# Gated DeltaNet's input weights: the second part of a tile made by an accumulating DMA instead of a VectorE subtraction

## The chip, the cores and the metric

The kernel runs on one core of one Trainium2 chip. The metric is the device time of one execution in microseconds (us), as the median of three runs. A profile of one execution goes with it: every instruction with its start, duration and the source line it came from, and every DMA.

The core's engines each take their own instructions in order. TensorE (PE in the profile, with its weight loads as PEld) multiplies, VectorE (DVE) and ScalarE (ACT) work elementwise, GpSimd (POOL) does small copies and issues some DMAs, and SyncE (SP) issues the other DMAs. They wait for each other through semaphores.

## The reference

Four decoder layers on 1024 positions of width 1024, in float32. The layers use HGRN2, sliding-window attention, gated DeltaNet and HGRN2 again. Only the third is touched:

```python
def gdn_mixer(h, w_in, w_out, conv_w, a_log, dt_bias, onorm_g):
    qkv, z, a, b = jnp.split(h @ w_in, [GD_QKV, GD_QKV + GD_VW, GD_QKV + GD_VW + GD_V_HEADS], axis=-1)
    qkv = jax.nn.silu(causal_conv(qkv, conv_w))
    q, k, v = jnp.split(qkv, [GD_QKW, 2 * GD_QKW], axis=-1)
    ...
    o = gated_delta_scan(q, k, v, beta, g)
    o = rmsnorm(o, onorm_g).reshape(B, T, GD_VW).astype(h.dtype)
    return (o * jax.nn.silu(z)) @ w_out
```

`h @ w_in` is the projection whose weights the change concerns: 1024 rows and 6176 columns, of which 6144 go through the loader described below.

## The kernel before

**Two-part products.** A float32 product is made of three fast TensorE matmuls. Each operand is split into a first part `hi`, the value rounded to the type `fp32r`, and a second part `lo`, what the rounding left. `mm3` (lines 215 to 220) adds three products: first parts by first parts (L218), the weight's first part by the activation's second (L219), and the weight's second part `w_lo` by the activation's first (L220).

**The weight loader.** `load_w` makes one tile of 128 partitions by 512 elements, 256 KB. SP fetches the raw tile into `w_raw` (L187), ACT writes `w_hi` (L189), and DVE writes `w_lo` = raw − hi (L190). There are three buffers for `w_raw`, which the tiles `ada_w` of another stream share, and four for each of `w_hi` and `w_lo`. Where a scale is given (output weights), L192 and L193 do the same; they are not changed.

**Projections.** `proj_fm` takes a column block of 128 outputs. Its weights are two tiles of four contraction steps each. For each half of the positions (512) it runs 8 steps of `mm3`, so 24 matmuls, 12 for each tile; then an evacuation reads the result from PSUM. Blocks of k, q and v go through a convolution (`conv`, L684 to L697), with small POOL copies of the three columns at a half's border (L678, L680, L687: `gd_xs`, `gd_halo`). Some blocks are run for both halves with one load of the weights, others for one half at a time: of the 64 block loads, 32 serve two halves and 32 serve one. That makes 128 tiles and 96 halves.

**Units.** DeltaNet's 16 heads are done in 8 units of two. For each unit `inverse` solves a triangular system: 31 steps of two DVE instructions (L837, L838), then a chain of small matmuls into `z_ps` (L866 to L894) with copies by ACT, DVE and POOL between them (POOL's are L860, L861, L870 and L886, on `gd_Z` and `gd_uq`). `scan` then steps through the eight chunks of 128 positions (L934 to L969), a chain of TensorE, DVE and ACT. `weave` mixes the instructions of a unit's scan, the next unit's inverse, the projections of later units, and `side`, which prepares the next layer's modulation with DVE (L444, reading `ada_w`).

**Order.** The program is written through a tile framework. It gives each instruction its engine, inserts the semaphores, and orders the instructions of each engine by priority and by the time at which it plans them to be ready. An instruction moved from one engine to another therefore changes the planned order on all of them. On the chip each engine then works through its list strictly in order.

The stage of the change runs from about 1077 us (first raw tile fetched, while the layer before still ends) to about 1890 us of the profiled span; the last DeltaNet unit and the output projection follow.

Of the kernel before, what the change touches and what calls it, by code (L numbers as in the profile page):

```python
# [10 lines left out]
F32 = mybir.dt.float32  # L11
# [4 lines left out]
AF = mybir.ActivationFunctionType  # L16
ALU = mybir.AluOpType
# [30 lines left out]
def drain(g):  # L48
    for _ in g:
        pass  # L50


def chain(*gs):
    for g in gs:
        yield from g


def take(g, n):
    for _ in range(n):
        c = next(g, None)  # L60
        if c is None:
            return
        yield c


def weave(tc, *streams):

    live = [[g, tot, b, e - b, b, pr] for g, tot, b, e, pr in streams]
    while live:
        s = min(live, key=lambda x: x[4])  # L70
        if s[5]:
            with tc.high_priority(offset=s[5]):
                c = next(s[0], None)
        else:
            c = next(s[0], None)
        if c is None:
            live.remove(s)
        else:
            s[4] += c * s[3] / s[1]


class Trunk:
    def __init__(self, ctx, tc, ins):
        self.ctx, self.tc, self.nc, self.ins = ctx, tc, tc.nc, ins
        pool = lambda name, bufs=1, **k: ctx.enter_context(tc.tile_pool(name=name, bufs=bufs, **k))
        self.const = pool("const")
        self.big = pool("big")
        self.wp = pool("wp")
        self.adap = pool("adap")
        self.sm = pool("sm")  # L90
        self.ps = pool("ps", space=PSUM)
        self.np_, self.pb, self.pw, self.pe = 0, 3, 0, 0
        self.dram = pool("dram", space=bass.MemoryType.DRAM)
        self.xd = self.dram.tile([D, T], F32, name="xd")
        self.od = [self.dram.tile([D * (1 + n), T], F32, name=f"od{n}") for n in range(2)]
        self.pd = self.dram.tile([D, T], F32, name="pd")
        self.zd = self.dram.tile([2 * D, T], F32, name="zd")
        self.hhi, self.hlo = [None, None], [None, None]
        self.x = [None, None]
        self.oo, self.pre, self.last, self.parts, self.due, self.more = {}, {}, iter(()), 0, set(), True  # L100
        self.piece = self.hold = self.turn = self.step = None


    def hslot(self, name):
# [71 lines left out]
    def load_w(self, src, scale=None, pool=None):  # L176

        nc, pool = self.nc, pool or self.wp
        shape = list(src.shape)
        raw = self.wp.tile([P, HT], F32, name="w_raw", tag="raw", bufs=RAW)  # L180
        hi = pool.tile([P, HT], F32R, name="w_hi", tag="whi", bufs=WB)
        lo = pool.tile([P, HT], F32R, name="w_lo", tag="wlo", bufs=WB)
        raw, hi, lo = (x[:, :math.prod(shape[1:])] for x in (raw, hi, lo))
        if len(shape) == 3:
            raw, hi, lo = (x.rearrange("p (a b) -> p a b", a=shape[1]) for x in (raw, hi, lo))
        with self.tc.high_priority(offset=self.pw):
            nc.sync.dma_start(raw, src)  # L187
            if scale is None:
                nc.scalar.copy(hi, raw)  # L189
                nc.vector.tensor_tensor(lo, raw, hi.bitcast(F32), ALU.subtract)  # L190
            else:
                nc.scalar.activation(hi, raw, AF.Copy, scale=scale)  # L192
                nc.vector.scalar_tensor_tensor(lo, raw, scale, hi.bitcast(F32), ALU.mult, ALU.subtract)  # L193
            n = self.tc.cur_priority
        self.tc.cur_priority = n + self.pw
        return hi, lo
# [379 lines left out]
    def gdn(self, i, side):  # L576
        nc, ins = self.nc, self.ins
# [6 lines left out]
        def tl(tag, dt=F32):  # L584
            return gp.tile([P, HT], dt, name=f"gd_{tag}", tag=tag, bufs=bufs[tag])
# [6 lines left out]
        raw = self.wp.tile([P, HT], F32, name="w_raw", tag="raw", bufs=RAW)[:, :KT * 32].rearrange("p (k n) -> p k n", k=KT)  # L592
# [119 lines left out]
        def proj_kq(u, dd, halves=((0, 1),)):  # L712

            if not dd:
                dd.update(k=[0, 0], q=[0, 0], kt=[0, 0], v={})
                dd["ms"] = gp.tile([P, 2 * C], F32, name="gd_ms", tag="ms", bufs=2)

            def ev_k(hf, ps):
                dd["k"][hf] = tl("k")
                conv(dd, hf, ps, 8 + u, dd["k"][hf])  # L720

                def turn():
                    pt = trans(dd["k"][hf], "ktr_ps")
                    dd["kt"][hf] = tl("kt")
                    nc.scalar.copy(dd["kt"][hf], pt)
                    sumsq(dd, pt, hf * NC)

                return turn

            def ev_q(hf, ps):  # L730
                dd["q"][hf] = tl("q")
                conv(dd, hf, ps, u, dd["q"][hf])
                return lambda: sumsq(dd, trans(dd["q"][hf], "qtr_ps"), C + hf * NC)

            for hv in halves:
                yield from self.proj_fm(w_in, D + u * P, ev_k, hv)
                yield from self.proj_fm(w_in, u * P, ev_q, hv)
                if hv == (0,):
                    yield from proj_z(u, dd, hv)
                    return  # L740
            self.turns()
            t8 = lambda name, n=C: gp.tile([P, n], F32, name="gd_" + name, tag=name, bufs=2 if name in ("r2", "gn") else 3)
            ms = dd["ms"]
            nc.vector.tensor_scalar(ms, ms, 0.25, EPS, ALU.mult, ALU.add)
            r = self.rsqrt(ms, 2 * C, "g", gp)

            ir, r2, sc = t8("ir"), t8("r2"), t8("sc")
            gm, gn, gw = (t8(n, 2 * C) for n in ("gm", "gn", "gw"))
            ac = lambda x: x.rearrange("p (a c) -> p a c", a=2)
            hs = slice(2 * u * C, 2 * (u + 1) * C)  # L750
            nc.vector.tensor_tensor(ir, ms[:, :C], r[:, :C], ALU.mult)
            nc.vector.tensor_tensor(r2, r[:, :C], r[:, :C], ALU.mult)
            nc.vector.scalar_tensor_tensor(ac(gm), r2[:, None, :].to_broadcast([P, 2, C]), 0.25, ac(beta[:, hs]), ALU.mult, ALU.mult)
            nc.vector.tensor_scalar(gn, gm, -1.0, None, ALU.mult)
            nc.vector.tensor_tensor(gw, gm, wl[:, hs], ALU.mult)
            nc.vector.tensor_scalar(sc, r[:, C:], 0.5 * P ** -0.5, None, ALU.mult)
            dd.update(ir=ir, gm=gm, gn=gn, gw=gw, sc=sc)
# [19 lines left out]
        def proj_z(u, dd, halves=(0, 1)):  # L777
            for a in range(2):
                def ev(hf, ps):
                    th = tl("tb")  # L780
                    nc.scalar.activation(th, ps, AF.Tanh, scale=0.5)
                    nc.vector.scalar_tensor_tensor(th, th, 1.0, ps, ALU.add, ALU.mult)
                    nc.sync.dma_start(place(self.zd, 2 * u + a, hf), th)

                yield from self.proj_fm(w_in, 4 * D + (2 * u + a) * P, ev, halves)
# [187 lines left out]
        w_out, od, on = ins["gd_out_w"][0], self.od[1], self.par[:, 74:75]  # L973
        ds = [dict() for _ in range(U)]
        self.parts = 4
        self.early(chain(proj_kq(0, ds[0], ((0,),)), proj_z(1, ds[1], (0,)), proj_z(2, ds[2], (0,))), EV)
        drain(self.last)
        decays()
# [4 lines left out]
        for u in range(U):  # L983
            cs = [proj_z(x, ds[x], hv) for x, *hv in ZL[u]]
            tot = 10400 * sum(len(z) - 1 for z in ZL[u])
            if u + 2 < U:
                cs.append(proj_kq(u + 2, ds[u + 2]))
                tot += 20800
            if u + 1 < U:
                cs.append(proj_v(u + 1, ds[u + 1]))  # L990
                tot += 20800
            st_ = [(scan(u, ds[u]), 18000, 0, 1, PR[0])]
            if u + 1 < U:
                st_.append((inverse(u + 1, ds[u + 1]), 28000, 0, 1, PR[1]))
            else:
                self.fill_x(0)
                cs += [self.out_load(od, 0, KT, 0, gp, "tmp", 2, (self.zd, "tb", bufs["tb"])), self.out_mm(i, w_out, 0, KT, 0, on), self.out_load(od, 0, KT, 1, gp, "tmp", 2, (self.zd, "tb", bufs["tb"]))]
                tot += 41600
            weave(self.tc, *st_, (chain(*cs), tot, 0, 1, 0), (take(side, NS[2]), NS[2], 0, 1, 0))
        drain(side)  # L1000
        st.close()
        st = ExitStack()
# [637 lines left out]
```

## Time and profile before

| what | value |
|---|---|
| median of three runs | 2658.29 us (2656.97 to 2660.67) |
| profiled execution, from its first to its last instruction | 2664.1 us |
| granted TensorE clock, mean of the span | 0.990 |
| `w_lo` by DVE (L190) between 1090 and 1910 us | 128 instructions, 87.8 us |
| `w_hi` by ACT (L189) in the same stretch | 128 instructions, 79.7 us |
| DMAs issued by POOL in the whole program | 56: 48 of `xd` at L142 and 8 of the rotary tables |

The profiled span is 5.8 us (0.2%) above the median of the runs that were not profiled; the profile holds no time outside its span. The profile's page gives busy time by engine, the span in 40 slices, the DMA queues, the chain of work that ended last, and the costliest groups of instructions. A group's row ends with the idle time that its engine had just before it and with what ended that idle time. The trace answers further questions by stretch of time, by line and by wait. A matmul's end is modelled: neighbouring matmuls overlap in the records, so a PE that is shown busy can still be waiting a little.

### The profile page before, as it was taken

The page shows a single profiled execution, that of the slowest core. Times are in us where ns is not written, and L with a number is a line of the kernel's source. Part 1 is how long each engine was busy: PE and PEld are TensorE (multiplying, and loading weights), DVE is VectorE, ACT ScalarE, POOL GpSimd, SP SyncE. Part 2 cuts the span into 40 slices and gives each one's busy share as a digit, 9 for nine tenths or more (in the row PEclk, how much of TensorE's full clock was granted, in tenths as well). Part 3 has the DMA queues.
Part 4 walks back from the last instruction along what each step waited for, and adds up shares of the span by engine and source line. Part 5 has one row for each costly group of instructions (what it writes and reads, how often), then busy time and mean ns, then how long its engine had stood idle before and what let it go on. Part 6 is the DMA issues. An engine that isn't in the chain of part 4 may idle for free.

```text
span 2664.1 us, 50723 instructions
## 1 busy us (share of the span) xinstructions
PE 2568.7 (96%) x18271; PEld 2046.2 (77%) x18271; DVE 2021.6 (76%) x5655; ACT 1323.5 (50%) x3467; POOL 105.7 (4%) x278
## 2 busy tenths in 40 slices
PE   7999999999999999999999999999999999999998
PEld 4777777778888877677877777778688877787777
DVE  5585788687697877768899999988776837368675
ACT  4443444443464655545666666666544534345352
POOL 0001000001000000101000100110000000000000
PEclk8999999999999999999999999999999999999999
DMA  7333343544233253334343444333576412122343
GB/s 261 98 114 90 116 143 115 173 128 129 67 103 104 72 160 112 95 110 111 106 123 84 118 118 119 83 97 93 174 235 188 123 48 77 42 82 64 124 139 116
DMA packets 395025, 309.96 MB, mean 116 GB/s; under 512 B 74851, under 2 KB 314902, under 8 KB 394774
## 3 DMA queue, kind: packets, MB, share of 16 engines
q1 hardware_dynamic: 390550, 293.09, 37.4%
q0 software_dynamic: 4224, 13.64, 1.6%
q8 instruction: 144, 2.36, 0.4%
q14 instruction: 107, 0.88, 0.1%
HBM read 245.75 MB, written 60.88 MB: 115 GB/s over the span
## 4 chain that ended last, share of the span: by engine, by line
PE 72%; DVE 14%; DMA 6%; ACT 5%; issue 2%; SPq 1%; DVEq 0%; ACTq 0%
PE proj_ps L218 10%; PE proj_ps L220 10%; PE proj_ps L219 10%; PE outp_ps L218 4%; PE outp_ps L219 4%; PE outp_ps L220 4%; PE projw_ps L219 2%; PE projw_ps L218 2%; PE projw_ps L220 2%; DVE gd_tb L690 1%; DVE w_lo L190 1%; PE projt_ps L219 1%; PE projt_ps L220 1%; PE pv_ps L1502 1%; PE projt_ps L218 1%
## 5 line engine op out<-in xcount | busy, mean ns | idle before, releaser
L218 PE MATMUL proj_ps<-hhi,w_hi 128*128 128x512 f32 x1664 | 676.0, 407 | 3.7 <-ACT gd_tb L688 3.3
L219 PE MATMUL proj_ps<-hlo,w_hi 128*128 128x512 f32 x1664 | 671.4, 404 | 0.0
L220 PE MATMUL proj_ps<-hhi,w_lo 128*128 128x512 f32 x1664 | 671.1, 403 | 0.0
L218 PEld LDWEIGHTS proj_ps<-hhi,w_hi 128*128 128x128 f32 x1664 | 314.6, 189 | 64.3 <-ACT gd_tb L688 5.9
L220 PEld LDWEIGHTS proj_ps<-hhi,w_lo 128*128 128x128 f32 x1664 | 314.1, 189 | 58.1 <-issue 0.4
L219 PEld LDWEIGHTS proj_ps<-hlo,w_hi 128*128 128x128 f32 x1664 | 314.6, 189 | 55.2 <-issue 0.9
L189 ACT CAST w_hi<-w_raw 128x512 fp32r<-128x512 f32 x352 | 214.5, 612 | 270.5 <-PE proj_ps L219 150.8
L190 DVE TENSOR_TENSOR w_lo<-w_raw,w_hi 128x512 fp32r<-128x512 f32 x352 | 236.5, 676 | 138.2 <-ACT w_hi L189 135.2
L218 PE MATMUL outp_ps<-o_hi,w_hi 128*128 128x512 f32 x576 | 229.8, 401 | 7.9 <-ACT o_hi L1314 7.0
L219 PE MATMUL outp_ps<-o_lo,w_hi 128*128 128x512 f32 x576 | 229.6, 399 | 0.4 <-DVE o_lo L1315 0.2
L220 PE MATMUL outp_ps<-o_hi,w_lo 128*128 128x512 f32 x576 | 228.0, 398 | 0.5 <-DVE w_lo L193 0.4
L192 ACT ACTIVATE w_hi<-w_raw,par 128x512 fp32r<-128x512 f32 (+1 forms) x136 | 94.8, 698 | 131.0 <-PE outp_ps L219 88.1
L690 DVE SCALAR_TENSOR_TENSOR gd_tb<-gd_xs,taps,gd_tb 128x512 f32<-128x512 f32 x192 | 145.7, 759 | 16.2 <-ACT gd_tb L688 12.5
L218 PEld LDWEIGHTS outp_ps<-o_hi,w_hi 128*128 128x128 f32 x576 | 109.4, 190 | 31.8 <-ACT o_hi L1314 9.7
L193 DVE SCALAR_TENSOR_TENSOR w_lo<-w_raw,par,w_hi 128x512 fp32r<-128x512 f32 (+1 forms) x136 | 96.9, 715 | 45.2 <-ACT w_hi L192 43.9
L444 DVE SCALAR_TENSOR_TENSOR ada_acc<-ada_w,par,ada_acc 128x512 f32<-128x512 f32 x154 | 114.9, 746 | 19.8 <-DMA ada_w<-in_ada_w_dram 18.8
L219 PEld LDWEIGHTS outp_ps<-o_lo,w_hi 128*128 128x128 f32 x576 | 109.4, 190 | 24.9 <-DVE o_lo L1315 3.0
L220 PEld LDWEIGHTS outp_ps<-o_hi,w_lo 128*128 128x128 f32 x576 | 109.1, 190 | 22.6 <-DVE w_lo L193 1.1
L219 PE MATMUL projt_ps<-w_lo,hhi 128*128 128x256 f32 x384 | 111.6, 292 | 2.2 <-DVE w_lo L190 2.2
L218 PE MATMUL projt_ps<-w_hi,hhi 128*128 128x256 f32 x384 | 111.0, 292 | 2.7 <-ACT w_hi L189 2.7
L220 PE MATMUL projt_ps<-w_hi,hlo 128*128 128x256 f32 x384 | 111.4, 292 | 0.0
L218 PE MATMUL projw_ps<-w_hi,hhi 128*128 128x512 f32 x256 | 102.8, 407 | 2.3 <-DVE hg_q L1032 2.3
(409 smaller groups left out, 5218.0 us busy)
## 6 DMA issues: line engine op xcount, KB each, us to landing
ada_w<-in_ada_w_dram SPq DMA_DIRECT2D x160, 256.0 KB, 2.8
w_raw<-in_hg_in_w_dram SPq DMA_DIRECT2D x136, 256.0 KB, 2.9
w_raw<-in_gd_in_w_dram SPq DMA_DIRECT2D x128, 256.0 KB, 3.0
o_in<-od SPq DMA_DIRECT2D x72, 256.0 KB, 3.7
x<-xd SPq DMA_DIRECT2D x64, 256.0 KB, 4.4
w_raw<-in_gd_out_w_dram SPq DMA_DIRECT2D x64, 256.0 KB, 3.1
xd<-x POOLq DMA_DIRECT2D x48, 256.0 KB, 2.9
w_raw<-in_sw_in_w_dram SPq DMA_DIRECT2D x48, 256.0 KB, 3.1
```

The source lines that it names most:

```text
L189: nc.scalar.copy(hi, raw)
L190: nc.vector.tensor_tensor(lo, raw, hi.bitcast(F32), ALU.subtract)
L192: nc.scalar.activation(hi, raw, AF.Copy, scale=scale)
L193: nc.vector.scalar_tensor_tensor(lo, raw, scale, hi.bitcast(F32), ALU.mult, ALU.subtract)
L218: mm(out, a[0], b[0], start=start, stop=False)
L219: mm(out, a[0], b[1], start=False, stop=False)
L220: mm(out, a[1], b[0], start=False, stop=stop)
L444: self.step = self.nc.vector.scalar_tensor_tensor(acc, w, c, acc, ALU.mult, ALU.add)
L690: last = nc.vector.scalar_tensor_tensor(y, xs[:, j:j + HT], w(j), y, ALU.mult, ALU.add)
L1502: self.tied([lambda b=b, a=a: nc.tensor.matmul(po[a * 64:(a + 1) * 64], vg[:, n + 1 - nkb + b, :], p4s[b][:, :, a, :], start=b == nkb - 1, ...
```

## The change

For the tiles of `gd_in_w` that are loaded while DeltaNet runs, DVE no longer takes part. ACT writes `w_hi` as before, then writes the negated first part into `w_lo` (`activation` with scale −1.0), and POOL issues a DMA from SBUF to SBUF that adds the raw tile onto it. A flag, `by_dma`, is set before the first early projections and cleared after the last unit's loop, so the other layers' tiles and the output weights keep their way.

```diff
+        self.by_dma = False
...
             nc.sync.dma_start(raw, src)
-            if scale is None:
+            if scale is None and self.by_dma:
+                nc.scalar.copy(hi, raw)
+                nc.scalar.activation(lo, hi.bitcast(F32), AF.Copy, scale=-1.0)
+                nc.gpsimd.dma_start(lo, raw, accum_op=ALU.add)
+            elif scale is None:
                 nc.scalar.copy(hi, raw)
                 nc.vector.tensor_tensor(lo, raw, hi.bitcast(F32), ALU.subtract)
...
         self.parts = 4
+        self.by_dma = True
         self.early(chain(proj_kq(0, ds[0], ((0,),)), proj_z(1, ds[1], (0,)), proj_z(2, ds[2], (0,))), EV)
...
             weave(self.tc, *st_, (chain(*cs), tot, 0, 1, 0), (take(side, NS[2]), NS[2], 0, 1, 0))
+        self.by_dma = False
         drain(side)
```

The added lines shift the numbers: in the changed kernel the three new steps are L190 (`w_hi`), L191 (negated copy) and L192 (DMA), and DeltaNet's lines are 5 higher (L837 is L842).

On DVE, inside the first inverse (`gd_A` holds the system, `gd_Tb` its growing inverse, `gd_tmp` the products), two `w_lo` stood among the steps. Before:

```order
L837 TENSOR_TENSOR gd_tmp<-gd_A,gd_Tb 128x121
L190 TENSOR_TENSOR w_lo<-w_raw,w_hi 128x512
L838 TENSOR_TENSOR gd_Tb<-gd_Tb,gd_tmp 128x11x11
L697 SCALAR_TENSOR_TENSOR gd_k<-gd_tb 128x512
L837 TENSOR_TENSOR gd_tmp<-gd_A,gd_Tb 128x110
L838 TENSOR_TENSOR gd_Tb<-gd_Tb,gd_tmp 128x10x11
L837 TENSOR_TENSOR gd_tmp<-gd_A,gd_Tb 128x108
```

After:

```order
L842 TENSOR_TENSOR gd_tmp<-gd_A,gd_Tb 128x121
L843 TENSOR_TENSOR gd_Tb<-gd_Tb,gd_tmp 128x11x11
L842 TENSOR_TENSOR gd_tmp<-gd_A,gd_Tb 128x110
L843 TENSOR_TENSOR gd_Tb<-gd_Tb,gd_tmp 128x10x11
L695 SCALAR_TENSOR_TENSOR gd_tb<-gd_xs,taps,gd_tb 128x512
L842 TENSOR_TENSOR gd_tmp<-gd_A,gd_Tb 128x108
```

The tile's instruction is gone from between the steps, and the convolution's instructions (L690, now L695; L697) stand elsewhere among them.

On ACT, around the fourth inverse's copy of `gd_Tc` (L848, now L853), the change puts a second instruction for each tile, with others between the two. Before:

```order
L189 CAST w_hi<-w_raw 128x512
L770 ACTIVATE gd_v<-vtr_ps,gd_ir 128x128
L848 COPY gd_Tc<-gd_tmp 128x16x2x16
L770 ACTIVATE gd_v<-vtr_ps,gd_ir 128x128 x3
L867 COPY gd_Z<-z_ps 32x16x32
```

After:

```order
L853 COPY gd_Tc<-gd_tmp 128x16x2x16
L715 ACTIVATE gd_tb,gd_ms<-qtr_ps 128x128
L693 ACTIVATE gd_tb<-proj_ps,taps 128x512
L190 CAST w_hi<-w_raw 128x512
L872 COPY gd_Z<-z_ps 32x16x32
L191 ACTIVATE w_lo<-w_hi 128x512
```

What moved: the tile's second part follows its first on the same engine, one instruction behind, here with the inverse's copy of `gd_Z` between them.

On POOL, at the first inverse's copies. Before:

```order
L680 COPY gd_xs<-gd_halo 128x3
L678 MEMSET gd_xs 128x3
L860 COPY gd_Z<-gd_Tc 32x16x32
L861 COPY gd_Z<-gd_Tc 32x16x32
L870 COPY gd_uq<-gd_Uc 32x16x32 x2
L886 COPY gd_uq<-gd_Uc 32x16x32 x2
L687 COPY gd_halo<-gd_xs 128x3
```

After:

```order
L192 DMA w_lo<-w_raw 128x512
L683 MEMSET gd_xs 128x3
L865 COPY gd_Z<-gd_Tc 32x16x32
L866 COPY gd_Z<-gd_Tc 32x16x32
L875 COPY gd_uq<-gd_Uc 32x16x32 x2
L891 COPY gd_uq<-gd_Uc 32x16x32 x2
L192 DMA w_lo<-w_raw 128x512 x9
L692 COPY gd_halo<-gd_xs 128x3
```

The DMAs stand in POOL's list before and behind the inverse's copies and the convolution's border copies: one ahead of them here, then nine in a row.

## The prediction

> **What bounds the kernel now.** I read the page's first lines, then the engines in 100 us stretches, then the groups by line, the waits and the DMA issues of DeltaNet's stretch. The page first:
>
> ```profile
> span 2664.1 us, 50723 instructions
> PE 2568.7 (96%) x18271; PEld 2046.2 (77%) x18271; DVE 2021.6 (76%) x5655; ACT 1323.5 (50%) x3467; POOL 105.7 (4%) x278
> PE 72%; DVE 14%; DMA 6%; ACT 5%; issue 2%; SPq 1%; DVEq 0%; ACTq 0%
> ```
>
> PE is busy for 96% of the span and holds 72% of the chain that ended last; DVE holds 14% of it. Four stretches from the middle of DeltaNet (busy time per engine, mean granted clock, DMA share, GB/s):
>
> ```profile
> 1290.00:1390.00 100.00, 96.85 (x684) 77.40 (x683) 91.36 (x258) 63.42 (x206) 8.70 (x24) 1.00 0.45 115
> 1390.00:1490.00 100.00, 98.01 (x693) 78.66 (x692) 93.35 (x286) 67.20 (x216) 7.12 (x21) 1.00 0.38 98
> 1490.00:1590.00 100.00, 97.57 (x687) 78.06 (x685) 92.19 (x270) 64.14 (x203) 9.77 (x21) 1.00 0.44 116
> 1590.00:1690.00 100.00, 97.71 (x689) 78.49 (x688) 92.97 (x270) 63.07 (x206) 8.56 (x23) 1.00 0.41 107
> sum 400.00, PE 390.14 PEld 312.61 DVE 369.86 ACT 257.83 POOL 34.16; mean PE 97.53 PEld 78.15 DVE 92.46 ACT 64.46 POOL 8.54
> ```
>
> PE is at 97.5% and full clock, DVE at 92.5%, ACT at 64.5%. A second engine at 92.5% looks like a bound, but what it costs is only the time in which PE stands still for it. PE's waits between 1110 and 1910 us (total us, times, longest):
>
> ```profile
> PE z_ps L883 <- DVE gd_uq L878: 7.4, 7, 1.7
> PE proj_ps L218 <- ACT gd_tb L688: 3.3, 4, 1.6
> PE vtr_ps L703 <- DVE gd_tb L697: 2.8, 6, 1.0
> PE S_ps L950 <- ACT gd_ws L946: 1.5, 3, 0.7
> PE w_ps L945 <- DVE gd_y L940: 1.4, 1, 1.4
> PE qtr_ps L703 <- DVE gd_q L697: 1.2, 2, 1.0
> PE ktr_ps L703 <- DVE gd_k L697: 0.9, 1, 0.9
> ...
> PE proj_ps L218 <- DVE gd_tb L782: 0.2, 1, 0.2
> ```
>
> Of the 17 rows 12 name DVE and sum to 16.9 us (13.7 in the first seven), and 5 name ACT and sum to 6.3. So at most some 23 us of 800 can come back from these two engines, whatever is taken from them. No row names `w_lo` or `w_hi` as PE's releaser: weights come in time.
>
> **What goes.** The loader's two steps, between 1090 and 1910 us:
>
> ```profile
> L190 DVE TENSOR_TENSOR w_lo<-w_raw,w_hi 128x512 fp32r<-128x512 f32 x128 | 87.8, 688 | 23.4 <-ACT w_hi L189 22.1 <-PE proj_ps L219 0.6 <-ACT gd_wg L960 0.3
> L189 ACT CAST w_hi<-w_raw 128x512 fp32r<-128x512 f32 x128 | 79.7, 625 | 72.2 <-PE proj_ps L219 60.4 <-DMA w_raw<-in_gd_in_w_dram 5.9 <-issue 2.9
> ```
>
> DVE loses 128 subtractions of 688 ns, 87.8 us, and the 22.1 us it stood behind `w_hi` at the head of its list. Over 800 us that is 11.0 us of work per 100, so DVE's free share in the middle goes from 7.5 to about 18.5%. Of PE's 16.9 us for DVE, 7.4 are the inverse's `z_ps` row: a chain of small matmuls and copies, each waiting for the one before, which a free DVE shortens only where the copy was queued. The other 9.5 us are queueing. I take them as proportional to busy share over free share (an estimate, the usual shape of a queue): 7.5/18.5 = 0.4 remains, **−5.7 us**. For the z row and weight loads I take another **−2 us**. The bounds of the whole term are 0 (PE's waits are chains, not queues) and −16.9.
>
> **What is added on ACT.** A negated copy of 128x512, as ACT does it already for another tile of that size:
>
> ```profile
> L696 ACT ACTIVATE gd_tb<-gd_tb 128x512 f32<-128x512 f32 x64 | 40.4, 632 | 50.9 <-DVE gd_tb L690 36.8 <-DVE rs_t L171 11.3 <-DVE rs_y L169 1.5
> ```
>
> 128 × 0.632 = 81 us, 10.1 per 100, so ACT goes from 64.5 to some 74.6% and its free share from 35.5 to 25.4. PE's 6.3 us for ACT grow by 35.5/25.4 − 1 = 0.4: **+2.3 us**. The bounds are 0 and +6.3 (doubled), since ACT's list is in order and the second copy may stand ahead of an evacuation, as in the rows ahead of `gd_Z` shown above. The copy itself waits for nothing but its `w_hi` and the slot that `w_hi` has waited for already.
>
> **What is added on POOL and the DMA engines.** The trace has no accumulating DMA and none from SBUF to SBUF. The nearest rows are POOL's own issues and the transfers of equal or double size (KB each, median us from issue to landing):
>
> ```profile
> L142 POOL DMA_DIRECT2D xd<-x x48 | 26.0, 542 | 1055.2 <-DVE x L572 802.5 <-DMA o_z<-zd 127.5 <-DVE x L1333 73.1
> DMA to landing us min/median/max: 2.3/2.9/4.5
> w_raw<-in_gd_in_w_dram SPq DMA_DIRECT2D x128, 256.0 KB, 3.0
> od<-sw_of SPq DMA_DIRECT2D x6, 512.0 KB, 3.8
> x_in<-in_x_dram SPq DMA_DIRECT2D x8, 512.0 KB, 9.1
> ```
>
> An issue holds POOL 0.54 us: 128 of them are 69 us, in 800 us where POOL is 8.5% busy, so they cost nothing as work. An accumulation reads two tiles and writes one, so it lies nearer to 512 KB than to 256: I take 3.8 us to landing, with the ends 2.3 and 9.1.
>
> **Is `w_lo` in time?** `w_hi` starts when PE has left the slot four tiles back. Then three tiles of work stand between it and its first use, 12 matmuls each where a block serves one half. A matmul comes every 0.23 us:
>
> ```profile
> 1135.53 0.39 PE L218 MATMUL proj_ps<-hhi,w_hi 128*128 128x512 f32 x1
> 1135.76 0.39 PE L219 MATMUL proj_ps<-hlo,w_hi 128*128 128x512 f32 x1
> ```
>
> 3 × 12 × 0.228 = 8.2 us, double where a block serves both halves, and more where inverse or scan matmuls lie between. The new way takes 0.62 (`w_hi`) + 0.63 (negated copy) + 0.5 (handoffs) + 3.8 = 5.6 us. It fits, with 2.6 us left for queueing on ACT and POOL. Before, DVE's queue used that room too: one `w_hi` ended at 1589.55 us, and its `w_lo` began at 1593.37, 3.8 us later, behind the inverse's steps:
>
> ```profile
> 1588.86 0.69 ACT L189 CAST w_hi<-w_raw 128x512 fp32r<-128x512 f32 x1
> 1593.37 0.68 DVE L190 TENSOR_TENSOR w_lo<-w_raw,w_hi 128x512 fp32r<-128x512 f32 x1
> ```
>
> So a DMA's latency takes the place of a queue's. I cost the lateness at 0, covered by these three tiles. With a landing of 9.1 us the way is 10.9, and 2.7 us are missing every four tiles (a slot's round): over the 64 one-half tiles 16 × 2.7 = **+43 us** if no other matmuls fill in, and about +16 if they fill two thirds.
>
> **Raw buffers.** A raw tile is now held until the DMA has read it, some 3 us longer. Its round is 3.0 (fetch) + 0.62 + 0.63 + 0.5 + 3.8 = 8.6 us against three tiles, 8.2 us, in the densest stretch: 0.4/3 = 0.13 us a tile, over 64 tiles at most +9. SP stands for the slots already:
>
> ```profile
> SPq L187 <- DVE w_lo L190: 94.0, 40, 16.0
> ```
>
> That wait will grow and hold back the `ada_w` fetches and stores queued behind it on SP. PE doesn't wait for those in this stretch, and the projections take 96 × 24 × 0.228 = 525 of the 800 us, so a third of the time is slack for the round. I take 0.
>
> At this place a rule speaks against the change. The L142 issues lasted 0.54 us beside a busy DVE, with no sign of a stall. The Trainium skill, page "SBUF — State Buffer", section "Who interferes with whom", says that DVE and GpSimd share a pair of ports. While DVE runs a copy, cast or tensor-scalar in its two-port mode, GpSimd can't write the descriptors of its DMAs; its example is a DMA of some 620 ns that took 3100. By that factor an issue of 0.54 would be 2.7 us, and the way 5.6 + 2.2 = 7.8 us, still under 8.2 but with no room for a queue. No run here shows it yet, and most wide DVE rows of DeltaNet are tensor-tensor forms, which the page excepts; it is one way into rival D.
>
> **Sum.** −5.7 − 2 + 2.3 + 0 = −5.4, about −6 with what DVE's 22.1 us of idling give the inverse. The profiled span is 2664.1 us, so the changed span would be about 2658. It stands 5.8 us above the median of the runs, 2658.29, and the profile holds nothing outside its span; taking the same difference for the median gives **2652 us**.
>
> **Rivals.**
>
> *A, the forecast: 2645 to 2653.* For it: DVE at 92.5%, PE's waits for DVE two and a half times those for ACT. Against it: the whole prize is 16.9 us.
>
> *B, no change: 2653 to 2663, likeliest 2657.* What DVE gives is taken by ACT, whose waits double (+6), or by PE's waits being chains. The z row is the largest of all and is such a chain. For it also that ACT already stands for PE's slot 60.4 us, so `w_hi` and the copy come in bunches.
>
> *C, slower by POOL's order: about 2682.* POOL takes its list in order, and a `w_lo` DMA may stand behind copies that wait for something late:
>
> ```profile
> POOL gd_halo L687 <- ACT gd_xs L684: 322.2, 27, 49.0
> POOL gd_Z L860 <- ACT gd_Tc L848: 69.1, 8, 50.1
> L870 POOL COPY gd_uq<-gd_Uc 32x512 f32<-32x512 f32 x16 | 11.5, 722 | 5.1 <-DVE gd_Uc L850 4.3
> L886 POOL COPY gd_uq<-gd_Uc 32x512 f32<-32x512 f32 x16 | 14.5, 906 | 0.9
> ```
>
> POOL waits up to 50.1 us at an inverse's first copy. Any `w_lo` DMA queued behind it starts only after that and the unit's copies (2 × 0.72 + 2 × 0.91 and the two of `gd_Z`). Against it: the wait lasts until DVE's inverse ends, but in the changed order, of the tiles loaded meanwhile, the DMAs stand ahead of the copies, and the first one behind them is used by PE 44 or more projection matmuls later (10 us) in seven units and 64 of all kinds (about 9) in the first. It decides where a copy comes later than planned by more than 9 − 5.6 = 3.4 us; with some 3 us more at each of 8 units it is +24.
>
> *D, slower by a slow DMA: 2667 to 2695.* It decides at a landing of about 8.2 − 1.75 = 6.5 us, then the +16 to +43 from above. For it: `x_in` took 9.1 at 512 KB. Against it: those eight were issued four at a time near the program's start, while the stores of 512 KB took 3.8:
>
> ```profile
> 3.05 1.85 SPq L312 DMA_DIRECT2D x_in<-in_x_dram  x4
> 25.14 5.20 SPq L312 DMA_DIRECT2D x_in<-in_x_dram  x4
> ```
>
>
> *E, the change doesn't do what it says* (DVE is freed, but its list is reordered so that the convolution or inverse comes later): within B's range, and counted there.
>
> **How the numbers follow.** A 0.42, B with E 0.31, C 0.13, D 0.14. The likeliest is A, so 2652. Range: below 2640 (all of 16.9 back, ACT for nothing) I leave 0.07, above 2682 (the harder half of C and D) 0.11. A measurement of this kernel can tell about 0.2%, 5 us, from no change. By that bound faster is 0.42, the same 0.31, slower 0.27.
>
> **What would show it.** Right: no `w_lo` on DVE between 1090 and 1910 us, DVE at about 81% in the four stretches, ACT at 74 to 75 with the copy near 632 ns; issues of 0.54 us with landings under 4.5; PE's waits for DVE at some 9 us in place of 16.9, those for ACT at 8 to 9, and none for the DMA of `w_lo`. Wrong by D: landings above 6.5 us, or issues of over a microsecond beside DVE's copies, and PE waiting at L220 for the DMA. Wrong by C: landings short, but issues that begin just after `gd_uq`'s copies, with PE waiting for them. Wrong by B: DVE freed as said while PE's waits keep their sum. A raw round that binds would show as `w_hi` waiting for the raw tile's DMA, 5.9 us before, by tens.

## The result, and the profile after

The changed kernel takes 2708.54 us (median of 4 runs, 2701.98 to 2714.94) against 2659.11 of the kernel before (2656.97 to 2660.67) on the same chip: a ratio of 1.0175, interval 1.0158 to 1.0193, so 42 to 51 us slower. The forecast was 6 us faster, in a range from 2640 to 2682. The page's first lines:

```profile
span 2700.3 us, 51023 instructions
PE 2577.0 (95%) x18271; PEld 2045.8 (76%) x18271; DVE 1958.0 (73%) x5527; ACT 1386.5 (51%) x3595; POOL 209.2 (8%) x406
PE 51%; issue 19%; DVE 15%; DMA 10%; ACT 4%; SPq 1%; POOL 0%; DVEq 0%; POOLq 0%; ACTq 0%
```

The profiled span is 36.2 us longer. That is less than the 49 us between the medians, because the profiled execution of the changed kernel was the fastest of its four, and the one of the kernel before lay above its median. DVE lost 63.6 us of work and the kernel gained nothing from it. PE's share of the chain fell from 72 to 51%, but this share doesn't measure the loss: the run e6 below loses 10.5 us and shows 59%. The stretches of DeltaNet (columns as before), with the two at its start, which the prediction left out:

```profile
1090.00:1190.00 100.00, 86.56 (x378) 65.56 (x377) 47.20 (x96) 53.01 (x114) 27.74 (x46) 0.98 0.72 163
1190.00:1290.00 100.00, 90.86 (x626) 73.53 (x625) 66.50 (x169) 61.74 (x168) 23.07 (x41) 0.97 0.67 147
1290.00:1390.00 100.00, 94.53 (x670) 74.75 (x670) 81.39 (x250) 67.39 (x209) 18.20 (x34) 1.00 0.62 141
1390.00:1490.00 100.00, 95.40 (x675) 75.70 (x675) 84.61 (x244) 71.24 (x221) 19.91 (x35) 1.00 0.61 142
1490.00:1590.00 100.00, 94.72 (x672) 74.34 (x672) 82.91 (x247) 70.74 (x216) 18.93 (x35) 1.00 0.62 143
1590.00:1690.00 100.00, 95.18 (x664) 76.41 (x663) 78.41 (x225) 65.26 (x195) 20.82 (x36) 0.98 0.63 145
```

DVE is at 78 to 85%, about as forecast, and ACT at 65 to 71 in place of the forecast's 74 to 75. PE is down in every stretch: by 2.3 to 2.9 points in the middle, more at the start. The last two columns tell what else moved: the DMA engines' share went from about 0.4 to 0.6 and 0.7. The two kernels in two stretches, before first:

```profile
1090.00:1290.00 200.00, 194.10 (x1108) 154.94 (x1108) 153.94 (x358) 103.33 (x270) 16.61 (x44) 0.99 0.41 115
1290.00:1890.00 600.00, 586.38 (x4314) 468.73 (x4313) 542.59 (x1577) 381.73 (x1209) 53.12 (x135) 1.00 0.41 107
```

```profile
1090.00:1290.00 200.00, 177.41 (x1003) 139.10 (x1002) 113.70 (x264) 114.75 (x281) 50.80 (x86) 0.97 0.70 155
1290.00:1890.00 600.00, 572.22 (x4036) 454.16 (x4035) 495.18 (x1480) 414.16 (x1273) 115.71 (x209) 1.00 0.60 138
```

PE loses 16.7 us of work in the first 200 us and 14.2 in the next 600, 30.9 of the 36.2. This pair of numbers is what the experiments below are read by. It is a rough measure: where the granted clock is lower, a matmul counts for more busy time (in e10 below 185 ns at 0.94, in e11 174 at 0.99), so it understates the loss there. PE's longest waits between 1110 and 1910 us:

```profile
PE proj_ps L225 <- DMA w_lo<-w_raw: 9.2, 6, 2.8
PE ktr_ps L708 <- DVE gd_k L702: 7.6, 5, 2.3
PE z_ps L888 <- DVE gd_uq L883: 6.7, 5, 3.1
PE w_ps L950 <- DVE gd_y L945: 3.9, 6, 1.0
```

PE now waits for `w_lo` (9.2 us, forecast none), and more than before for a DVE that has more time: the 13 rows that name DVE sum to 28.1 us, against 16.9 before and a forecast of 9. Those that name ACT sum to 8.3, as forecast. What DVE, ACT and SP wait for from DMAs points to why (between 1090 and 1910 us; total, times, longest):

```profile
DVE gd_tmp L814 <- DMA gd_tmp<-dd: 18.9, 10, 7.0
DVE ada_acc L449 <- DMA ada_w<-in_ada_w_dram: 15.6, 12, 3.1
ACT w_hi L190 <- DMA w_raw<-in_gd_in_w_dram: 41.1, 24, 5.3
SPq L188 <- DMA w_lo<-w_raw: 235.1, 75, 19.8
SPq L463 <- DMA w_lo<-w_raw: 61.8, 24, 6.0
```

Before, DVE's two rows were:

```profile
DVE gd_tmp L809 <- DMA gd_tmp<-dd: 4.2, 7, 2.5
DVE ada_acc L444 <- DMA ada_w<-in_ada_w_dram: 0.7, 1, 0.7
```

In the run e5 below, which has no added DMA and loses nothing, they are:

```profile
DVE gd_tmp L813 <- DMA gd_tmp<-dd: 14.9, 12, 4.8
DVE ada_acc L448 <- DMA ada_w<-in_ada_w_dram: 2.2, 3, 1.4
```

So DVE stands for the decays (`gd_tmp` from the scratch `dd`) and for the other stream's weights. The first of these waits comes mostly with a freed DVE and is no sign of the loss; the second, 15.6 us against 2.2, is new. ACT stands for raw tiles, 41.1 us in place of 5.9, which is the sign that the prediction named for a raw round that binds. SP stands for raw buffers, since `L188` (the raw fetch) and `L463` (the `ada_w` fetch) now wait until an accumulation has landed. The added steps themselves:

```profile
L192 POOL DMA_DIRECT2D w_lo<-w_raw x128 | 108.2, 848 | 453.4 <-ACT w_lo L191 262.9 <-PE w_ps L966 54.1 <-ACT gd_qse L946 48.0
L191 ACT ACTIVATE w_lo<-w_hi 128x512 fp32r<-128x512 f32 x128 | 81.1, 634 | 1.8 <-PE proj_ps L225 0.6
w_lo<-w_raw POOLq DMA_DIRECT2D x128, 256.0 KB, 3.9
```

The negated copy took what was forecast (634 ns), the issue 0.85 us in place of 0.54, the landing 3.9 us against 3.8.

At the start the raw buffers' round (from one fetch into a buffer to the next) shows plainly. Three pieces of the timeline, of SP's, ACT's and POOL's lists:

```profile
1098.74 2.62 SPq L188 DMA_DIRECT2D w_raw<-in_gd_in_w_dram  x2
1103.75 0.62 ACT L190 CAST w_hi<-w_raw 128x512 fp32r<-128x512 f32 x1 [3.93 <-DMA w_raw<-in_gd_in_w_dram]
1105.34 0.88 POOL L192 DMA_DIRECT2D w_lo<-w_raw  x1 [5.39 <-ACT w_lo L191]
1108.76 2.78 SPq L188 DMA_DIRECT2D w_raw<-in_gd_in_w_dram  x2
1112.19 0.62 ACT L190 CAST w_hi<-w_raw 128x512 fp32r<-128x512 f32 x1 [5.31 <-DMA w_raw<-in_gd_in_w_dram]
```

SP issues two fetches from 1098.74 and the next two only from 1108.76, when accumulations have landed: 10.0 us for two tiles, 5 us each, where PE needs 2.7 for a tile that serves one half (12 × 0.228). ACT stands for the raw tile 3.9 and 5.3 us. It is two tiles and not three because the third raw buffer holds the narrow tile of the last 32 columns, fetched at 1068.4 us (L598) and read by ACT only at 1116.1 (L599, `gd_wab`). The kernel before has that too, but makes six fetches there in 13.1 us, where the changed kernel makes four in 12.8.

### The profile page after: what moved, and what is told of

It is laid out like the page before. It is cut to its first block, busy times and chain, and to the rows that moved or that the text cites. A ratio compares the mean times of both kernels' runs of the same rounds, so it can differ in the third digit from the quotient of the medians.

```text
span 2700.3 us, 51023 instructions
## 1 busy us (share of the span) xinstructions
PE 2577.0 (95%) x18271; PEld 2045.8 (76%) x18271; DVE 1958.0 (73%) x5527; ACT 1386.5 (51%) x3595; POOL 209.2 (8%) x406
## 3 DMA queue, kind: packets, MB, share of 16 engines
q1 hardware_dynamic: 390550, 293.09, 36.4%
## 4 chain that ended last, share of the span: by engine, by line
PE 51%; issue 19%; DVE 15%; DMA 10%; ACT 4%; SPq 1%; POOL 0%; DVEq 0%; POOLq 0%; ACTq 0%
PE proj_ps L225 7%; PE proj_ps L223 7%; PE proj_ps L224 7%; PE outp_ps L225 4%; PE outp_ps L224 4%; PE outp_ps L223 4%; PE projw_ps L224 2%; PE projw_ps L223 2%; PE projw_ps L225 2%; DVE gd_tb L695 2%; DMA w_lo<-w_raw 2%; DMA ada_w<-in_ada_w_dram 2%; DMA w_raw<-in_gd_in_w_dram 1%; DMA gd_tmp<-dd 1%; DMA w_raw<-in_hg_in_w_dram 1%
## 5 line engine op out<-in xcount | busy, mean ns | idle before, releaser
L195 DVE TENSOR_TENSOR w_lo<-w_raw,w_hi 128x512 fp32r<-128x512 f32 x224 | 148.7, 668 | 112.9 <-ACT w_hi L194 111.6
L695 DVE SCALAR_TENSOR_TENSOR gd_tb<-gd_xs,taps,gd_tb 128x512 f32<-128x512 f32 x192 | 143.5, 747 | 37.0 <-ACT gd_tb L693 32.1
L192 POOL DMA_DIRECT2D w_lo<-w_raw x128 | 108.2, 848 | 453.4 <-ACT w_lo L191 262.9
L190 ACT CAST w_hi<-w_raw 128x512 fp32r<-128x512 f32 x128 | 79.3, 621 | 86.8 <-PE proj_ps L224 44.7
```

The source lines that it names most:

```text
L192: nc.gpsimd.dma_start(lo, raw, accum_op=ALU.add)
L695: last = nc.vector.scalar_tensor_tensor(y, xs[:, j:j + HT], w(j), y, ALU.mult, ALU.add)
```

## The experiments

The letters here are not those of the prediction's rivals. The theories at first: A, the copies on ACT; P, POOL's list in order; O, the planner's changed order; R, the raw buffers that the DMA holds; D, the DMA's whole way. Later came L, a late `w_lo`; T, the load that the added DMAs put on the engines that all transfers share; S, the raw buffers shared with `ada_w`; and Q, SP's list in order. "PE lost" is PE's busy time from 1090 to 1290 and from 1290 to 1890 us, against the kernel before (194.10 and 586.38). Differences are between medians on the same chip, with the interval of the ratio.

**One part at a time: e1 to e7.** The lines at the three steps of the loader:

```diff
# e1_dram: the raw tile is added from DRAM
-nc.gpsimd.dma_start(lo, raw, accum_op=ALU.add)
+nc.gpsimd.dma_start(lo, src, accum_op=ALU.add)
# e2_pool: subtraction on GpSimd, no copy, no DMA
+nc.gpsimd.tensor_tensor(lo, raw, hi.bitcast(F32), ALU.subtract)
# e3_act: the copy on ACT, the addition on DVE
-nc.gpsimd.dma_start(lo, raw, accum_op=ALU.add)
+nc.vector.tensor_tensor(lo, raw, lo.bitcast(F32), ALU.add)
# e4_late: by_dma set after proj_kq(0, ds[0], ((1,),))
# e5_nodma: the DMA left out
# e6_tiny: eight columns
+nc.gpsimd.dma_start(lo[:, 0, :8], raw[:, 0, :8], accum_op=ALU.add)
# e7_halo: L683, L685, L692 on nc.vector
```

> The accumulating DMA reads the tile a second time from DRAM in place of the raw buffer, so a raw buffer is free as soon as ACT has written w_hi; all else is as in the changed kernel (about 2709 us against 2659 before). Theory R (the raw buffers' round, fetch to landing of the accumulation, binds and holds ACT up at w_hi): the early stretch 1090 to 1290 gets its 17 us back and ACT's wait for the raw tile falls from 41 us to under 15; 2665 to 2680. Theory P (POOL's list in order: the convolution's border copies stand behind DMAs that wait for ACT) and theory A (the 81 us added on ACT) and theory O (the planner's other order): no change, 2700 to 2715, since none of them depends on what the DMA reads.

> The second part is a subtraction on GpSimd: no negated copy on ACT, no accumulating DMA, DVE freed all the same. A subtraction of 128x512 on GpSimd takes perhaps 1.2 us (the copies of 32x512 took 0.7 to 0.9), so the raw buffer is free about 3 us sooner than with the DMA. Theory R: the early loss goes; theory A: the rest goes too; both 2650 to 2668. Theory P: POOL has more work than with the DMA and still stands behind ACT; 2685 to 2715.

> ACT writes the negated first part as in the change, and DVE adds the raw tile to it: no DMA, POOL as before, DVE as loaded as before, the raw buffer free after about 2 us. It has only the cost of the added ACT copies, and a planned order near that of before. Theory A: most of the loss stays, 2690 or more. Theories R and P: 2658 to 2672.

> The first 28 tiles (the early projections, dense in weights) keep DVE; the other 100 go by DMA. By the profiles, 17 of the 36 us lost by the profiled span arise up to 1290 us. Theory R with the early stretch as its place: 2678 to 2692. If the loss is spread over all tiles (theories P, A): about 100/128 of it stays, 2695 to 2702. If the early lag also causes the later losses, under 2670.

> The accumulating DMA is left out, so the second part holds only the negated first part: DVE is freed and ACT loaded as in the change, but nothing waits for a DMA, POOL and the raw buffers are free. (Before 2663 in the last comparison, the changed kernel about 2709, 2694 with the raw buffer released early.) Theory D (the DMA's way costs all of it: its issue on POOL, its latency, the raw buffers): 2645 to 2660, so a freed DVE is worth up to 15 us. Theory O (a planner that sees DVE free puts its steps just in time, and on the chip DVE, ACT and PE then stand at heads of lists): 2680 to 2695, the loss stays without any DMA.

> The accumulating DMA adds only the first 8 of the 512 columns (4 KB of 256), so issue, semaphores and POOL's order stay while the bytes go and the landing falls from 3.9 to perhaps 2 us. If bytes, landing time and the raw buffers' round cost: 2655 to 2672. If the issue on POOL, its order or the planner's order cost: 2690 to 2710.

> The change as it is, but the convolution's border copies (three columns) and clears are made by DVE, so that POOL's list holds beside the DMAs only the inverse's copies. Theory P (these copies stand behind DMAs that wait for ACT, or the DMAs behind them): 2675 to 2690. Otherwise 2705 to 2715; 96 short DVE instructions of under 0.1 us cost at most a few us.

| run | us, before | difference | ratio, interval | PE lost |
|---|---|---|---|---|
| e3_act | 2662.85, 2663.30 | −0.5 | 0.9988 to 1.0009 | 0.6, −1.1 |
| e5_nodma | 2660.44, 2664.31 | −3.9 | 0.9978 to 0.9996 | −0.6, −0.9 |
| e6_tiny | 2674.77, 2664.31 | +10.5 | 1.0028 to 1.0058 | 2.8, −1.1 |
| e1_dram | 2693.82, 2663.30 | +30.5 | 1.0095 to 1.0126 | 7.8, 12.6 |
| e4_late | 2700.44, 2663.30 | +37.1 | 1.0125 to 1.0155 | 6.0, 14.6 |
| e7_halo | 2712.13, 2664.31 | +47.8 | 1.0162 to 1.0192 | 10.8, 16.0 |
| e2_pool | 2743.23, 2663.30 | +79.9 | 1.0276 to 1.0310 | not used |

A falls: with 128 copies on ACT and all else as before, nothing changes. O falls, as far as this kernel's plan shows it: without the DMA, with DVE free in the planner's eyes, the kernel is 3.9 us *faster* (its second parts hold only the negated first part, so its output is not the layer's; e6's neither). That is what the relief of DVE is worth, copies on ACT included. P's border copies fall with e7, where DVE makes them. The DMA costs all of it, and e6 halves the question: with 4 KB in place of 256, the same 128 issues (0.85 us each) and the raw buffers still held until a landing, only 10.5 us stay (2674.8, some 3 us above the range set for bytes and landing), and PE loses no busy time after 1290 us. e1 and e4 were misses of theory R by its own numbers: with the raw buffer free after `w_hi` the loss after 1290 us stays, and with the early tiles kept from the DMA too; e4's 2700.4 lies in the range set for a loss spread over all tiles. But in e1 ACT's wait for the raw tile falls from 41.1 to 1.6 us, and PE's early loss from 16.7 to 7.8, so R may be about half of the early loss. (e4 kept 20 tiles, not 28 as expected: 108 DMAs are in its trace.) e1 also changed two things, since its DMA reads the tile in pieces of 512 bytes: the DMA engines' share rose to 0.86 and 0.70. e2 is slower still, and why is not settled; its profile was taken at a granted clock of 0.706.

**The raw buffers: e8 to e11.**

```diff
# e9_k4
-GB = {"k": 5,
+GB = {"k": 4,
# e8_k4_raw4: the same, and for every fourth tile
+raw = self.gp.tile([P, HT], F32, name="w_raw", tag="graw", bufs=1)
# e10_hold: the loader as before, and then
+nc.gpsimd.memset(raw[:, 0, 0:1], 0.0)
+nc.gpsimd.dma_start(scr, raw)
# e11_traffic
+nc.gpsimd.memset(raw[:, 0, 0:1], 0.0)
+nc.gpsimd.dma_start(scr, lo.bitcast(F32))
```

> The change with one raw buffer more: every fourth input tile takes a raw buffer of its own, whose 2 KB per partition come from the k tiles (4 buffers in place of 5; the next run has that alone). Theory R (the raw buffers' round binds while the DMA holds them): a third more buffers relieve most of it, 2670 to 2685 or 20 us and more under the next run. Theory T (the DMA engines' added load slows every transfer) or L (w_lo itself comes late): within 5 us of the next run.

> The change with 4 buffers for k tiles in place of 5 and nothing else, the measure for the run before. By all theories as the changed kernel, 2705 to 2715, or a few us more where a k tile's buffer is late.

> As before the change (subtraction on DVE), and then, for the same tiles, GpSimd clears one column of the raw buffer and issues a DMA of the raw buffer to a scratch in DRAM. w_lo is not later, ACT and DVE have what they had, but the raw buffer is held some 3.5 us longer and 256 KB more are moved. Theory R: 25 us or more over before (2664), and at least 15 over the next run. Theory L: within 6 of before. Theory T: as the next run.

> As the run before, except that the DMA reads w_lo in place of the raw buffer: the same issues, bytes and moments, but the raw buffer is free after the subtraction and GpSimd's clear. Theory T: 15 us or more over before. Theory R: under 10 us over before.

| run | us, before | difference | ratio, interval | PE lost |
|---|---|---|---|---|
| e8_k4_raw4 | 2726.99, 2664.24 | +62.8 | 1.0210 to 1.0246 | 13.8, 25.5 |
| e9_k4 | 2732.76, 2664.24 | +68.5 | 1.0235 to 1.0274 | 16.7, 25.7 |
| e10_hold | 2691.34, 2664.24 | +27.1 | 1.0089 to 1.0122 | 12.7, 3.5 |
| e11_traffic | 2684.02, 2664.24 | +19.8 | 1.0051 to 1.0104 | 7.4, 5.8 |

A fourth raw buffer is worth some 6 us, not 20. (Taking a buffer from k costs some 20 us beside the change, which was not expected; in this pair it is in both.) L isn't needed for the losses of e10 and e11, where `w_lo` is made as before; in the changed kernel it is the 9.2 us of PE at the start. Holding the raw buffer to the landing (e10 against e11) costs 7 us more by the medians, though the two intervals overlap, and by PE's busy time it is lost before 1290 us. With e1 this speaks for R as a real, early and smaller part; its size is not settled. e11, however, was not traffic alone. SP's waits in it:

```profile
SPq L188 <- POOL w_raw L192: 164.0, 71, 16.2
```

POOL's clear holds the raw buffer as well, so e11 separates the two theories badly.

**The shared weights: e12 to e14, and the queue: e15 to e17.**

```diff
# e12_no_ada (on the change), e13_no_ada_b (on before), e14_late_no_ada (on e4)
-weave(self.tc, *st_, (chain(*cs), tot, 0, 1, 0), (take(side, NS[2]), NS[2], 0, 1, 0))
+weave(self.tc, *st_, (chain(*cs), tot, 0, 1, 0))
# e15_raw_on_pool (on the change), e16_late_raw_on_pool (on e4), e17_before_raw_on_pool (on before)
-nc.sync.dma_start(raw, src)
+(nc.gpsimd if self.by_dma else nc.sync).dma_start(raw, src)
```

> The change, with the next layer's modulation (its ada_w fetches and DVE's steps on them) taken out of the units' weave and done behind it; the next run is the kernel before with the same edit. Theory S (the late part of the loss is the shared raw ring: ada_w, fetched into the same three buffers, comes late and DVE stands at ada_acc with the inverse's and scan's steps behind it): no growth of the lag after 1290 us, and 15 to 25 us between this run and the next in place of about 45. Theory T (the added traffic slows the others' transfers by itself): 35 us or more between them.

> The kernel before with the modulation behind the units, the measure for the run ahead of this one and the one behind it; some 20 to 60 us over before, since 40 fetches and DVE steps then stand alone.

> The change for all but the first 28 tiles, and without the modulation in the weave. If the loss is the raw ring in two places, the dense early tiles and the shared ada_w, this has neither: within 8 us of the run ahead of it. By theory T 25 us or more over it.

> The change, with the raw fetches of the same 128 tiles issued by POOL in place of SP: the buffers are held as long as before, but the transfers on SP (the decays' gd_tmp from dd, gd_A, ada_w) no longer stand behind a fetch that waits for a buffer. Theory Q (SP's list in order is how the held buffers reach DVE and PE): DVE's waits for gd_tmp and ada_w fall from 18.9 and 15.6 us to under 8 each, the lag no longer grows after 1290 us, 2680 to 2692 (the dense early tiles' own round stays, some 17 us). Theory T (the added traffic slows transfers by itself): these waits stay, 2700 or more.

> As the run ahead of it, but the first 28 tiles by the old way with DVE (their fetches on SP). Theory Q with the early round: both are taken away, 2664 to 2675 against 2700 for the first 28 tiles kept alone. Theory T: 2690 or more.

> The kernel before with the raw fetches of the 128 tiles issued by POOL, the measure for both runs ahead of it, and a try at a faster kernel, since SP stands 94 us for a raw buffer there too. If these waits cost before as well: 2650 to 2658. If they are covered: 2660 to 2668. If POOL's border copies hold the fetches back: over 2670.

| run | us, before | ratio, interval | against its measure | PE lost to its measure |
|---|---|---|---|---|
| e12_no_ada | 2772.21, 2666.00 | 1.0386 to 1.0422 | +36.4 | 14.9, 7.9 |
| e13_no_ada_b | 2735.78, 2666.00 | 1.0247 to 1.0282 | | |
| e14_late_no_ada | 2757.35, 2666.00 | 1.0326 to 1.0360 | +21.6 | 5.0, 6.9 |
| e15_raw_on_pool | 2731.13, 2661.86 | 1.0242 to 1.0279 | +49.1 | 17.4, 15.5 |
| e16_late_raw_on_pool | 2720.99, 2661.86 | 1.0188 to 1.0230 | +38.9 | 5.4, 21.0 |
| e17_before_raw_on_pool | 2682.08, 2661.86 | 1.0052 to 1.0090 | | |

Without `ada_w` the change costs 36.4 us in place of 49, some 13 less. That doesn't show S. By the numbers set, e12 met T; the two profiled executions are 43.4 us apart (2777.5 and 2734.1), more than the 36.2 of the change; and taking `ada_w` out also takes its traffic away, so that the DMA share after 1290 us is 0.54 in place of 0.60. Whether `ada_w` carries part of the loss through the shared buffers, through slow transfers or at all stays open. e14, with neither the early tiles nor `ada_w`, still lost 21.6, nearer to T's 25 than to S's 8. (e13 lay 70 us over before, above the 20 to 60 expected.)

Theory Q fell outright. With the raw fetches on POOL the change costs 49.1 and, for the late tiles, 38.9, as much as with SP, and in e15 DVE's waits for `gd_tmp` and `ada_w` stay at 16.7 and 20.0 us. SP's order is not how the loss reaches DVE. As a faster kernel e17 is a miss: it is 20.2 us slower than before, with no byte added, and ACT stands 19.9 us for raw tiles in place of 5.9. So what stands in POOL's list can cost by itself, where an engine waits for it.

**Load alone: e18.**

```diff
# the loader as before, and then
+for x in (hi, lo):
+    scr = self.dram.tile([P, 4, P], F32, name="scr", tag="scr", bufs=8)
+    nc.gpsimd.dma_start(scr, x.bitcast(F32))
```

> The kernel before, with two stores to a scratch in DRAM added for each of the 128 tiles, issued by POOL, one of w_hi and one of w_lo (2 x 256 KB, 2 x 0.54 us of POOL). ACT, DVE and the raw buffers are as before: nothing added touches the raw buffer (in e11 POOL's clear did, and SP stood 164 us for it). The DMA engines get about as much work as the accumulation gives them (0.84 us of all 16 for a plain transfer of 256 KB against 1.58 for an accumulated one). Theory T (traffic by itself): 12 us or more over before. The held raw ring: under 6 us over before, DVE's wait for gd_tmp under 8 us.

It takes 2691.97 us, 28.5 over before (ratio 1.0081 to 1.0118), with PE losing 10.3 and 9.6 us. Its two stretches, and SP's longest wait, which was 94.0 in the kernel before:

```profile
1090.00:1290.00 200.00, 183.76 (x1033) 146.13 (x1032) 142.60 (x329) 92.91 (x239) 64.00 (x132) 0.96 0.69 222
1290.00:1890.00 600.00, 576.78 (x4067) 456.97 (x4066) 532.25 (x1569) 380.14 (x1212) 137.42 (x290) 1.00 0.59 173
SPq L188 <- DVE w_lo L191: 91.2, 42, 15.7
```

The DMA share is that of the changed kernel (0.69 and 0.59 against 0.70 and 0.60), though more bytes are moved (222 and 173 GB/s against 155 and 138). No raw buffer is held, ACT and DVE have their old work, and over half of the loss is there. The transfers of the three kernels tell how (median us from issue to landing), before:

```profile
w_raw<-in_gd_in_w_dram SPq DMA_DIRECT2D x128, 256.0 KB, 3.0
zd<-gd_tb SPq DMA_DIRECT2D x32, 256.0 KB, 2.3
od<-gd_of SPq DMA_DIRECT2D x128, 64.0 KB, 1.8
gd_A<-ablk SPq DMA_DIRECT2D x16, 256.0 KB, 4.8
```

After the change:

```profile
w_raw<-in_gd_in_w_dram SPq DMA_DIRECT2D x128, 256.0 KB, 3.2
zd<-gd_tb SPq DMA_DIRECT2D x32, 256.0 KB, 3.3
od<-gd_of SPq DMA_DIRECT2D x128, 64.0 KB, 2.4
gd_A<-ablk SPq DMA_DIRECT2D x16, 256.0 KB, 5.5
```

And with the two stores, whose other half is as before:

```profile
w_raw<-in_gd_in_w_dram SPq DMA_DIRECT2D x128, 256.0 KB, 4.1
zd<-gd_tb SPq DMA_DIRECT2D x32, 256.0 KB, 3.6
od<-gd_of SPq DMA_DIRECT2D x128, 64.0 KB, 2.7
gd_A<-ablk SPq DMA_DIRECT2D x16, 256.0 KB, 6.2
DVE gd_tmp L816 <- DMA gd_tmp<-dd: 13.6, 11, 3.6
DVE ada_acc L451 <- DMA ada_w<-in_ada_w_dram: 10.8, 11, 2.4
```

These four land 0.2 to 1.0 us later after the change, and 0.9 to 1.4 later with the two stores alone. (`zd` takes 3.0 us in e6 too, where the other three are as before or sooner, so it is the weakest of the four.) DVE has its old work in e18, so the kernel before is the measure here, and all its waits for DMAs sum to 36.5 us between 1090 and 1910 us, against 9.5; PE's waits for DVE sum to 31.5, against 16.9.

Two other ways for e18 to lose are small by its waits. DVE stands 2.1 us for POOL's instructions (0.5 before) and PE not at all, so the 256 issues in POOL's list hold back little. The stores hold `w_hi` and `w_lo` longer, for which ACT and DVE stand 5.9 us, but PE waits for neither part. So T is shown for this much: the DMA load costs 22 to 31 us where no raw buffer is held, by PE's waits mainly through transfers for which DVE stands. It also fits that PE's loss after 1290 us goes with the DMA share there: none at 0.41 to 0.44 (e3, e5, e6), 3.5 and 5.8 us at 0.51 and 0.49 (e10, e11), 6.9 and 7.9 at 0.56 and 0.54 (e14 and e12, against their own measure), and 9.6 to 16.0 at 0.59 and 0.60 (e18, the change, e4, e7). The late loss of e1 is 12.6 at 0.70; e8, e9, e16 and e17 lose more than their shares would give.

## Why the prediction was wrong

**What bounds the kernel** was right: PE does, and DVE's 92.5% cost little. DVE's relief and ACT's cost were forecast at −7.7 + 2.3 = −5.4; e5 measured −3.9 for both, e3 about 0 for ACT alone. The sign and the smallness of the prize held. In e5 PE's waits for DVE fell to 13.3 us, not to 9, and those for ACT stayed at 6.1. The two terms also don't follow the rule that the prediction names: busy share over free share would leave 0.36 of DVE's queueing, not 0.4, and add 3.9 us for ACT, not 2.3; the free share alone was used.

**The way to `w_lo`** was right in its parts (634 ns, landing 3.9 us) but for the issue, 0.85 in place of 0.54. "I cost the lateness at 0" was wrong: PE waits for it 9.2 us, all between 1117 and 1176 us. Late raw tiles are a cause, but not shown to be the only one, since e1, where they come in time, still has 4.6 us of these waits.

**Raw buffers: "I take 0"** was wrong. The reason given, that a third of the time is slack for the round, is an average, and dense tiles stand together before 1290 us. The round was put at 8.6 us against three tiles; at the start it took 10.0, with two buffers going round and not three. Its size there: e1, which frees the buffer early, loses 8.9 us less of PE than the change, e10 5.3 more than e11, and e6 2.8 with a short landing. The sentence that SP's wait would hold back `ada_w` and "PE doesn't wait for those in this stretch" left out a step: DVE stands for them, 15.6 us, and PE waits for DVE. What that step costs is not settled (13 us less by e12's medians, nothing by its profile).

**"What is added on POOL and the DMA engines"** is the step that failed. It priced an issue on POOL and the new DMA's own landing, and nothing else. The sum has no term for what 128 more transfers do to the others, that is, this cost was put at nothing without a reason. The profile had the start of it: a share of 0.38 to 0.45 that was quoted, and a software queue whose 56 transfers took 0.76 us of all 16 engines each (1.6% of 2664 us by 56). That queue's share rose from 1.6 to 9.1%; before, and after:

```profile
q0 software_dynamic: 4224, 13.64, 1.6%
```

```profile
q0 software_dynamic: 22656, 47.20, 9.1%
```

7.5% of 2700 us by 128 tiles is 1.6 us of all engines for each, about twice that of a plain transfer. e18, with 256 stores at 0.7 us ((8.3 − 1.6)% of 2691 by 256), gives the size of the term that was missing: +28.5. For the change it is an estimate, since the change makes the other transfers less late than e18 does and its DMA stays in SBUF, where the stores of e18 go to DRAM.

By parts: −3.9 (e5), +28.5 (e18), and from e5 to e6 +14.4 for issue, short landing and held buffers, together +39 of the 49 measured. The parts come from kernels with different plans, issues on POOL are in two of them, and a late transfer under load also holds its raw buffer longer, so the sum is rough and the other 10 us are not assigned. PE's 9.2 us for `w_lo` are a candidate: e18 has none, e6 0.2. What stays open as well is which of the slowed transfers costs most (only `ada_w` was taken out).

Of the rivals, D said that a slow DMA would be 16 to 43 us, by its own landing over 6.5 us; it landed in 3.9, and slowed the others. (Its 16 is a third of 43, which is 14; and C's 2682 adds 24 to no change, where D adds to the forecast.) C is not borne out: PE's six waits for `w_lo` lie between 1117 and 1176 us, before the first inverse's copies at 1266.6, and e7 cleared the border copies. B's form, the gain given back on ACT, is excluded by e3.

## What to carry to other kernels

Work moved from a compute engine to a DMA can be paid for by the other transfers of that stage: look at the DMA share there, count the engine time of the new transfers, and ask which engines stand at the head of their lists for a transfer that just came in time. Relieving an engine at 92% was worth 4 us here, since PE's waits for it were 2% of the stage. And an average slack says nothing of the stretch where the tiles stand closest; work a buffer's round out there, and count which buffers of the ring really go round.

## What the runs showed of the hardware

- Landing times grew before the DMA engines were full: at a mean share of 0.6 to 0.7 (e18; 0.41 before) the 64 KB store `od` went from 1.8 to 2.7 us, and `w_raw` from 3.0 to 4.1.
- The accumulating DMA from SBUF to SBUF cost POOL more to issue than a plain one to DRAM, 0.85 us against 0.54, whether it moved 256 KB or 4 (e6: 850 ns), and 1.28 us when its source lay in DRAM in pieces of 512 bytes (e1). It took about twice the DMA engines' time of a plain store. No run parts the accumulation from the number of packets, which by the queue's counts was 144 for one such DMA, 80 for a plain store and 528 in e1.
- Nothing was seen of GpSimd's descriptors being held up by DVE, as the rule of the Trainium skill (page "SBUF — State Buffer", section "Who interferes with whom") would have it for DVE's copies, casts and tensor-scalar forms: the 128 issues took 828 to 1139 ns, the 17 that overlapped such a DVE instruction at most 852, and the DVE groups kept their means (759 and 747 ns for `gd_tb` with `gd_xs`).
